# Projection work handed out in quarter pieces, and in another order, in a hybrid HGRN2 and SSD mixer

## The chip, the cores and the metric

The kernel runs on one core of a Trainium2 chip. Its engines run at the same time, each through its own list of instructions in order: TensorE (PE, with its weight loads shown as PEld), VectorE (DVE), ScalarE (ACT), GpSimd (POOL) and SyncE (SP, which here only issues DMAs). They wait for each other on semaphores. The metric is the device time of one execution in microseconds. Lower is better.

## The reference, cut to what matters

One layer, one sequence of L = 1024 latent tokens with 256 context tokens ahead of them, model width 1024. Everything starts from one projection of the modulated input:

```python
u = h @ w_in_l
aq, af_f, af_b, ai, ag, bz, bxbc, bdt_f, bdt_b, gate_a, gate_b = jnp.split(u, IN_SPLITS, axis=-1)
ya = hgrn2_branch(aq, af_f, af_b, ai, ag, ...)          # 4 heads, gated linear recurrence, both directions
yb = ssd_branch(bz, bxbc, bdt_f, bdt_b, ...)            # 4 groups of 4 heads, Mamba-2 scan, both directions
merged = jax.nn.sigmoid(gate_a) * (ya @ wpa) + jax.nn.sigmoid(gate_b) * (yb @ wpb)
return merged @ wo
```

The change lies mostly in the second branch. For one of its four groups:

```python
xbc = jax.nn.silu(dwconv_centred(xbc, conv_w, conv_b, n_rows))     # blocks x, B and C, 5 taps
u  = einsum('bktgn,bktgr,bktgrp->bkgrnp', bc, exp(cum_last - cum), x_dt)   # state each chunk adds
y  = einsum('bktgn,bktgr,bkgrnp->bktgrp', cc, exp(cum), s_prev)            # from earlier chunks
   + einsum('bktsg,bktsgr,bksgrp->bktgrp', cb, lmat, x_dt)                 # inside the chunk
y  = group_rms((y_f + y_b + d_skip * xh) * silu(z)) * norm_w               # norm of the group
```

All arithmetic is float32. A projection product is made of three products of halves, high by high, low by high and high by low.

## The kernel before

Channels lie on the 128 partitions and tokens along a row. A projection of 128 channels (`proj`, L196) runs over eight k-tiles for each part of the tokens: two parts of 512, and for some blocks a third part of 256 context tokens. With three products for each k-tile (`mm3`, L174, whose lines are L178 to L180) a part of 512 tokens is 24 products of 128x512. This text calls such a part a **grain**. `GRAIN` is its 512 tokens, and a part of 256 counts as half a grain.

The kernel has two long stages, the recurrence of the first branch (L697) and the scan of the second (L951), then the output products `pa`, `pb` and `fo`. In both stages two sorts of work share TensorE. The **scan** is a chain of small products between which the other engines work. The **fill** is a queue of projections that later work needs. Each is a Python generator. `Fill.window` (L93) steps the scan, adds up the weights that it yields times a rate, and steps the fill until what the fill yields has used that up. So the order in which the program is written alternates pieces of scan and of fill, and a piece of fill is as long as what the fill generator emits between two of its yields. `Fill.until(name)` (L88) runs the fill up to the end of a named entry without counting it against the rate. A scheduler then makes each engine's list from this order, with some instructions moved ahead (`ahead`), and where a ring of buffers has none free it puts the instruction later.

In the second stage each group g goes through `b_window` (L932). Its scan (`b_scan`, L761) transposes B (`bb`), makes the products of C and B (`cb`), transposes x (`bx`), makes nine state steps (`bu` on TensorE from `xw` on POOL, L808 to L811), and then 16 **y steps**. A y step, one half j of the group and one chunk t, goes through four stages (L837 to L870) which `LAGS` (L38) writes 0, 1, 2 and 4 steps late:

- `loads`: POOL issues the DMA of tile `L`, 256 KB from DRAM.
- `exponents`: POOL issues the DMA of tile `e`, 256 KB. DVE takes a minimum on `L` (L843). ACT makes four exponentials on it (L846).
- `products`: POOL multiplies `e` by C (L851). DVE multiplies `L` by `CB` (L852).
- `y_matmuls`: TensorE makes the eight products of the step (L867) from `L` and `e`.

The tiles `L` and `e`, the `xw` and the tiles of the norm take their buffers from one ring of 12 (`w2`, L716). `b_out` (L900) is the first half of the norm of the group before: it waits in the program for that group's z projections (`fill.until`), squares on ACT, adds on POOL (L909), sums over partitions on TensorE (`bss`, L913). `b_scale` (L919) is the second half, on DVE. `OUT1` and `OUT2` (L35) say after how many steps of the scan they stand. `FILL_B` (L34) is the rate of each group.

The fill of group g, in this order (L951 to L961): one `gb` block (the second branch's merge gate), the z blocks of group g-1, more `gb` blocks, and the four blocks B, C, x0 and x1 of group g+1. In grains, for g = 1 and 2: gb 2, z 4, B 2.5, C 2, x 5, together 15.5. Group 0 has 13.5 and group 3 has 16 (its own z comes last, in L962 to L967).

Of the kernel before, what the change touches and what calls it, by code (L numbers as in the profile page):

```python
# [33 lines left out]
FILL_B = (0.75, 0.86, 0.86, 0.93)  # L34
OUT1, OUT2 = 3, 4  # L35
# [68 lines left out]
def hybrid(tc, x, c, ctx, c_ctx, w_mod, b_mod, w_in, lb_logits, a_norm_w, conv_w, conv_b, dt_bias,  # L104
# [13 lines left out]
    with root:  # L118
# [77 lines left out]
        def proj(col, parts, name, w=None):  # L196

            hi, lo = w or w_col(col, name)
            for t0, n in parts:
                acc = pj(f"{name}_{t0}")  # L200
                mm3(acc[:, :n], [((hi[:, k, :], lo[:, k, :]), hsl(k, t0, n)) for k in range(KT)])
                yield t0, n, acc[:, :n]

        def proj_k(col, parts, name):
# [22 lines left out]
        with ExitStack() as st:  # L227
# [180 lines left out]
            for t0, n, acc in proj(0, parts_a[1:], "i0", w=w_i):  # L408
                iT0[t0] = get_kt(f"iT0_{t0}")
# [15 lines left out]
        def a_proj(h, u, pre=None):  # L425
            if pre is None:
                Tt = get_T(f"T{h}")
                for d, o in ((0, O_FF), (1, O_FB)):
                    for t0, n, acc in proj(o + h * P, parts_a, f"f{d}{h}"):
                        with ahead():  # L430
                            S.activation(Tt[:, d, t0:t0 + n], acc, AF.Sigmoid)
                        yield n / GRAIN
# [8 lines left out]
            for t0, n, acc in gen:  # L441
                if pre is None:
# [9 lines left out]
                yield n / GRAIN if pre is None else 0.1  # L452
            u["v"] = vt
            q = gt("q", 2, [L], f"q{h}")
            for t0, n, acc in proj(O_Q + h * P, parts_l, f"q{h}"):
                with ahead():
                    S.copy(q[:, t0:t0 + n], acc)
                yield n / GRAIN
            u["q"] = q

        def a_gate(h, u):
            for t0, n, acc in proj(O_G + h * P, parts_l, f"g{h}"):
                with ahead():
# [3 lines left out]
                yield n / GRAIN  # L467
# [116 lines left out]
        def gate_proj(o, dst, b, alloc, name, proj=proj):  # L584
            for t0, n, acc in proj(o + b * P, parts_l, f"{name}{b}"):
                with ahead():
# [3 lines left out]
                yield n / GRAIN  # L590
# [149 lines left out]
        def b_proj(g, u):  # L740
            xc = bt_("xc", 2, [2, L], f"xc{g}")
            xcc = bt_("xcc", 1, [2, LC], f"xcc{g}")
            Bc = bt_("bc", 3, [L], f"B{g}")
            Bcc = bt_("bcc", 1, [LC], f"Bc{g}")
            Cc = bt_("bc", 3, [L], f"C{g}")
            for blk, main, side in ((8 + g, Bc[:], Bcc[:]), (12 + g, Cc[:], None),
                                    (2 * g, xc[:, 0, :], xcc[:, 0, :]), (2 * g + 1, xc[:, 1, :], xcc[:, 1, :])):
# [344 lines left out]
```

## Time and profile before

| What | Value |
|---|---|
| Median of 3 runs | 1297.26 us (1296.8 to 1297.93) |
| The profiled execution's own time | 1292.7 us |
| Its span | 1290.9 us |
| PE busy | 1230.7 us (95%), mean granted clock 0.981 |
| DVE / ACT / POOL busy | 740.8 us (57%) / 547.2 us (42%) / 239.1 us (19%) |
| DMA | 137.01 MB, mean 106 GB/s |

The span is what the profile sees of the execution. Its own time has 1.8 us more around it, and the median of the runs shown lies 4.6 us above that one execution. Busy shares are means over stages that differ much, so the rows below cut the span into stages. PEclk is TensorE's granted clock as a share of 2.4 GHz. An arrow in a row reads out<-in by the names of the tiles. What stands in brackets at the end of a row is the idle time of the engine just before it, and what ended that.

### The profile page before, as it was taken

How to read it: one execution, taken by the hardware profiler on the slowest of the kernel's cores; microseconds unless marked ns; L12 is line 12 of the kernel's file. 1: busy time of each engine (PE TensorE's matmuls, PEld its weight loads, DVE VectorE, ACT ScalarE, POOL GpSimd, SP SyncE). 2: the span in 40 equal slices, each digit the busy share in tenths (PEclk: the TensorE clock that was granted, in tenths of full speed). 3: DMA queues.
4: the chain of work that ended last, by engine and by line, in shares of the span. 5: the costliest groups of instructions: out<-in, count | busy, mean ns of one | idle time of the engine just before them, and what ended most of it. 6: DMA issues, size and time to landing. Idle time of an engine off the chain costs nothing.

```text
span 1290.9 us, 18817 instructions
## 1 busy us (share of the span) xinstructions
PE 1230.7 (95%) x7624; PEld 1010.6 (78%) x7624; DVE 740.8 (57%) x988; ACT 547.2 (42%) x864; POOL 239.1 (19%) x264
## 2 busy tenths in 40 slices
PE   5999999999999999999889997999799979999997
PEld 2778888888888888887778886888688857888886
DVE  2427555833745723637762886288625665575568
ACT  2436344433343323334663556355646854312110
POOL 1220000000000000025520554066405560000000
PEclk8999999999999999999999998999899989999999
DMA  9511312112112222115631545145534655663312
GB/s 319 185 41 33 99 34 92 42 33 68 34 33 68 74 66 92 49 57 128 144 84 47 140 116 122 50 126 128 140 99 139 162 141 179 234 255 108 146 41 97
DMA packets 126837, 137.01 MB, mean 106 GB/s; under 512 B 15568, under 2 KB 102288, under 8 KB 126752
## 3 DMA queue, kind: packets, MB, share of 16 engines
q1 hardware_dynamic: 107744, 102.09, 25.2%
q0 software_dynamic: 18656, 33.69, 11.1%
q8 instruction: 60, 0.98, 0.3%
q14 instruction: 25, 0.20, 0.1%
q10 hardware_dynamic: 352, 0.05, 0.0%
HBM read 115.55 MB, written 20.19 MB: 105 GB/s over the span
## 4 chain that ended last, share of the span: by engine, by line
PE 76%; DVE 7%; issue 6%; POOL 5%; DMA 3%; ACT 1%; POOLq 0%; SPq 0%; DVEq 0%; ACTq 0%
PE f L180 3%; PE f L178 3%; PE x L178 3%; PE f L179 3%; PE x L179 3%; PE x L180 3%; PE pl L500 2%; POOL e L851 2%; PE z L178 2%; PE z L180 2%; PE pb L178 2%; PE pb L180 2%; PE fo L180 2%; PE fo L179 2%; PE z L179 2%
## 5 line engine op out<-in xcount | busy, mean ns | idle before, releaser
L851 POOL TENSOR_TENSOR e<-e,C 128x512 f32<-128x512 f32 x64 | 92.3, 1444 | 126.4 <-DMA e<-ecum_d 120.1
L846 ACT ACTIVATE L<-L,BIA 128x128 f32<-128x128 f32 x256 | 81.4, 390 | 58.6 <-DVE L L843 49.5
L808 POOL TENSOR_TENSOR xw<-xtc,WU 128x512 f32<-128x512 f32 x8 | 8.3, 1045 | 496.8 <-ACT xtc L794 496.8
L843 DVE TENSOR_TENSOR L<-L,CU 128x512 f32<-128x512 f32 x64 | 52.6, 823 | 51.3 <-DMA L<-cum_d 32.0
L867 PE MATMUL yi<-L,xt 128*64 128x128 f32 x512 | 42.7, 290 | 26.5 <-issue 15.0
L867 PEld LDWEIGHTS yi<-L,xt 128*64 128x64 f32 x512 | 29.5, 141 | 37.8 <-issue 20.6
L726 DVE SCALAR_TENSOR_TENSOR xc<-x,par,xc 128x496 f32<-128x496 f32 (+1 forms) x64 | 47.0, 734 | 18.5 <-ACT xc L723 17.7
L852 DVE TENSOR_TENSOR L<-L,CB 128x512 f32<-128x512 f32 x64 | 54.3, 855 | 3.9 <-ACT L L846 3.9
L178 PE MATMUL fo<-wo,mh 128*128 128x512 f32 x128 | 50.2, 392 | 0.0
L867 PE MATMUL yi<-e,St 128*64 128x128 f32 x512 | 42.6, 290 | 7.7 <-POOL e L851 5.8
L180 PE MATMUL fo<-wo,mh 128*128 128x512 f32 x128 | 49.8, 389 | 0.0
L179 PE MATMUL fo<-wo,ml 128*128 128x512 f32 x128 | 49.8, 389 | 0.0
L492 ACT COPY KX<-K 128x1024 f32<-128x1024 f32 x28 | 31.9, 1140 | 41.2 <-DVE K L511 40.4
L511 DVE TENSOR_TENSOR K<-K,T 128x1280 f32<-128x1280 f32 x28 | 46.4, 1658 | 3.5 <-ACT KX L492 1.6
L542 DVE SCALAR_TENSOR_TENSOR S<-S,T,ub 128x128 f32<-128x128 f32 x64 | 22.2, 348 | 43.6 <-PE ub L532 23.6
L898 DVE TENSOR_TENSOR xc<-xc,z 128x512 f32<-128x512 f32 x16 | 13.2, 825 | 55.2 <-ACT z L887 55.1
L833 POOL DMA_DIRECT2D e<-ecum_d x64 | 39.5, 617 | 8.3 <-PE yi L867 8.2
L503 DVE COPY_PREDICATED PD<-mk,pl 128x512 f32<-128x512 uint8 x24 | 17.7, 739 | 39.3 <-PE pl L500 25.6
L867 PEld LDWEIGHTS yi<-e,St 128*64 128x64 f32 x512 | 32.5, 146 | 9.4 <-POOL e L851 7.4
L513 DVE TENSOR_TENSOR Q<-Q,T 128x1024 f32<-128x1024 f32 x28 | 37.6, 1344 | 3.2 <-PE pl L500 3.2
L833 POOL DMA_DIRECT2D L<-cum_d x64 | 39.3, 614 | 1.0 <-PE bu L811 0.6
L500 PEld LDWEIGHTS pl<-Q,KX 128*64 128x64 f32 x896 | 30.1, 138 | 9.2 <-issue 8.7
(996 smaller groups left out, 3766.1 us busy)
## 6 DMA issues: line engine op xcount, KB each, us to landing
L<-cum_d POOLq DMA_DIRECT2D x64, 256.0 KB, 5.5
e<-ecum_d POOLq DMA_DIRECT2D x64, 256.0 KB, 5.2
wm<-in_w_mod_dram SPq DMA_DIRECT2D x16, 512.0 KB, 7.9
xt<-in_x_dram SPq DMA_DIRECT2D x8, 512.0 KB, 7.6
ga_d<-ga SPq DMA_DIRECT2D x16, 256.0 KB, 2.1
gb_d<-gb SPq DMA_DIRECT2D x16, 256.0 KB, 2.0
m<-ga_d SPq DMA_DIRECT2D x8, 512.0 KB, 6.1
gbt<-gb_d SPq DMA_DIRECT2D x8, 512.0 KB, 7.4
```

What stands on the lines that cost most here:

```text
L178: T.matmul(dst, ah, bh, start=(first and i == 0), stop=False)
L179: T.matmul(dst, al, bh, start=False, stop=False)
L180: T.matmul(dst, ah, bl, start=False, stop=(last and i == n - 1))
L500: T.matmul(pl[rows_, t * HP:(t + 1) * HP], KX[:, o:o + HP], qx, start=True, stop=True)
L511: V.tensor_tensor(kv, kv, sub(Ta, lv, [[w, NA // w], [NA - lv, 2], [0, lv]]), ALU.mult)
L726: V.scalar_tensor_tensor(d3[:, :, a:z], r3[:, :, a + o:z + o], cw_col(t, blk), d3[:, :, a:z], ALU.mult, ALU.add)
L833: G.dma_start(t_[:].rearrange("p a b c -> p (a b c)"), bass.AP(src.tensor, src.offset, [[NQT * BH * 2 * QT, REP], [0, P // REP], [1, 4 * Q ...
L843: V.tensor_tensor(Lm, Lm, sub(CU[:], t * BH + h0, [[1, 2], [NT * BH, 2], [0, P]]), ALU.min)
L846: S.activation(Lm[:, h, d, :], Lm[:, h, d, :], AF.Exp, bias=BIA[:, d, t, h0 + h:h0 + h + 1])
L851: G.tensor_tensor(C4, C4, Cc[:, ts].unsqueeze(1).broadcast_to([P, 4, P]), ALU.mult)
L852: V.tensor_tensor(Lm, Lm, CB[:, :, ts].unsqueeze(1).broadcast_to([P, 2, 2, P]), ALU.mult)
L867: T.matmul(yi[h * 64:(h + 1) * 64, o], a, r, start=(k == 0), stop=(k == 3))
```

## The change

Four things change. First, `proj` yields after every second k-tile, so a grain leaves the queue in four pieces of six products. The last z block, made by `proj_k`, yields likewise. Every user of a projection passes these yields on and counts a quarter of a grain for each. Second, the fill of a group has another order: B and C of the next group, z of the group before, the `gb` blocks, then x0 and x1 of the next group. `b_proj` takes its tiles when the first part of a block is done, not all at the start. Third, the norm of the group before stands after 8 steps of the scan and not 3, and its second half 3 steps later and not 4. Fourth, the rates of the four groups go from 0.75, 0.86, 0.86 and 0.93 to 0.74, 0.64, 0.64 and 0.8.

```diff
-FILL_B = (0.75, 0.86, 0.86, 0.93)
-OUT1, OUT2 = 3, 4
+FILL_B = (0.74, 0.64, 0.64, 0.8)
+OUT1, OUT2 = 8, 3
...
                 acc = pj(f"{name}_{t0}")
-                mm3(acc[:, :n], [((hi[:, k, :], lo[:, k, :]), hsl(k, t0, n)) for k in range(KT)])
+                for k in range(KT):
+                    mm3(acc[:, :n], [((hi[:, k, :], lo[:, k, :]), hsl(k, t0, n))], first=(k == 0), last=(k == KT - 1))
+                    if k % 2 and k < KT - 1:
+                        yield t0, n, None
                 yield t0, n, acc[:, :n]
...
             for t0, n, acc in proj(O_G + h * P, parts_l, f"g{h}"):
+                if acc is None:
+                    yield n / GRAIN / 4
+                    continue
...
-                yield n / GRAIN
+                yield n / GRAIN / 4
...
         for g in range(BG):
-            add_gb(1)
+            if g + 1 < BG:
+                fill.add(b_proj(g + 1, ub_[g + 1], ("B", "C")), f"b{g + 1}")
+            else:
+                add_gb(1)
             if g:
                 fill.add(z_proj(g - 1, ub_[g - 1]), f"z{g - 1}")
-            add_gb(GATES[g] - 1)
+            add_gb(GATES[g] - (g + 1 == BG))
             if g + 1 < BG:
-                fill.add(b_proj(g + 1, ub_[g + 1]), f"b{g + 1}")
+                fill.add(b_proj(g + 1, ub_[g + 1], ("x0", "x1")), f"b{g + 1}")
```

What this does to the lists of the engines is shown at three places of group 1. In the names, `L1_0_3` is the tile `L` of group 1, half 0, chunk 3, `e1_0_3` the tile `e` of the same step, and the last number is a buffer's.

TensorE at the first y steps, before: the end of a part of x4, three y steps in a row, and the next part, of which the first product is shown.

```order
L180 MATMUL x4_512_5932<-hl7_96,x4h_5865 128x512
L867 MATMUL yi1_0_0_5973<-L1_0_0_5862,xt1_5483 64x128 x4
L867 MATMUL yi1_0_0_5973<-e1_0_0_5903,St1_5664 64x128 x4
L867 MATMUL yi1_0_0_5973<-L1_0_1_5901,xt1_5483 64x128 x4
L867 MATMUL yi1_0_0_5973<-e1_0_1_5912,St1_5664 64x128 x4
L867 MATMUL yi1_0_0_5973<-L1_0_2_5910,xt1_5483 64x128 x4
L867 MATMUL yi1_0_0_5973<-e1_0_2_5923,St1_5664 64x128 x4
L178 MATMUL x4_1024_6020<-hc0_97,x4h_5865 128x256
```

And now:

```order
L180 MATMUL x4_0_5888<-hl5_94,x4h_5883 128x512
L902 MATMUL yi1_0_0_5929<-L1_0_0_5845,xt1_5454 64x128 x4
L902 MATMUL yi1_0_0_5929<-e1_0_0_5855,St1_5531 64x128 x4
L178 MATMUL x4_0_5888<-hh6_87,x4h_5883 128x512
L179 MATMUL x4_0_5888<-hh6_87,x4l_5884 128x512
L180 MATMUL x4_0_5888<-hl6_95,x4h_5883 128x512
L178 MATMUL x4_0_5888<-hh7_88,x4h_5883 128x512
L179 MATMUL x4_0_5888<-hh7_88,x4l_5884 128x512
L180 MATMUL x4_0_5888<-hl7_96,x4h_5883 128x512
L902 MATMUL yi1_0_0_5929<-L1_0_1_5853,xt1_5454 64x128 x4
L902 MATMUL yi1_0_0_5929<-e1_0_1_5873,St1_5531 64x128 x4
```

Every y step now has a quarter of a grain behind it, where three steps stood in a row with a whole part between such rows.

POOL at the same y steps, before: `DMA` rows are the loads it issues, the others its products.

```order
L851 TENSOR_TENSOR e1_0_0_5903<-e1_0_0_5903,C1_4637 128x512
L851 TENSOR_TENSOR e1_0_1_5912<-e1_0_1_5912,C1_4637 128x512
L833 DMA L1_0_3_5921<-cum_d_79 128x1x512
L833 DMA e1_0_2_5923<-ecum_d_80 128x1x512
L833 DMA L1_0_4_5962<-cum_d_79 128x1x512
L833 DMA e1_0_3_5964<-ecum_d_80 128x1x512
L851 TENSOR_TENSOR e1_0_2_5923<-e1_0_2_5923,C1_4637 128x512
L851 TENSOR_TENSOR e1_0_3_5964<-e1_0_3_5964,C1_4637 128x512
```

And now:

```order
L886 TENSOR_TENSOR e1_0_0_5855<-e1_0_0_5855,C1_4625 128x512
L868 DMA e1_0_2_5897<-ecum_d_80 128x1x512
L886 TENSOR_TENSOR e1_0_1_5873<-e1_0_1_5873,C1_4625 128x512
L868 DMA L1_0_4_5918<-cum_d_79 128x1x512
L868 DMA e1_0_3_5920<-ecum_d_80 128x1x512
L886 TENSOR_TENSOR e1_0_2_5897<-e1_0_2_5897,C1_4625 128x512
L868 DMA L1_0_5_5951<-cum_d_79 128x1x512
L868 DMA e1_0_4_5953<-ecum_d_80 128x1x512
L886 TENSOR_TENSOR e1_0_3_5920<-e1_0_3_5920,C1_4625 128x512
```

Before, the load of e1_0_2 and its product have no other product between them; now the load stands one product earlier.

POOL ahead of the first load of group 1, before: the adds of the norm of group 0 (`sq`) and the nine `xw`, of which the last five follow the four shown in the same way.

```order
L909 TENSOR_TENSOR sq0_0_0_5646<-sq0_0_0_5646,sq0_0_1_5647 128x512
L808 TENSOR_TENSOR xw1_0_5665<-xtc1_5484,WU_106 128x512
L909 TENSOR_TENSOR sq0_1_0_5655<-sq0_1_0_5655,sq0_1_1_5656 128x512
L808 TENSOR_TENSOR xw1_1_5702<-xtc1_5484,WU_106 128x512
L808 TENSOR_TENSOR xw1_2_5709<-xt1_5483,WU_106 128x512
L808 TENSOR_TENSOR xw1_3_5716<-xt1_5483,WU_106 128x512
```

And now, the last rows ahead of the first load and that load:

```order
L947 TENSOR_TENSOR sq0_0_0_5759<-sq0_0_0_5759,sq0_0_1_5760 128x512
L843 TENSOR_TENSOR xw1_5_5783<-xt1_5454,WU_106 128x512
L843 TENSOR_TENSOR xw1_6_5796<-xt1_5454,WU_106 128x512
L947 TENSOR_TENSOR sq0_1_0_5768<-sq0_1_0_5768,sq0_1_1_5769 128x512
L843 TENSOR_TENSOR xw1_7_5812<-xt1_5454,WU_106 128x512
L843 TENSOR_TENSOR xw1_8_5832<-xt1_5454,WU_106 128x512
L868 DMA L1_0_0_5845<-cum_d_79 128x1x512
```

The second add, which needs all z blocks of group 0, stood seven `xw` and more ahead of the first load and now stands two ahead of it.

## Rows read from the trace of the kernel before

**Rows 1.** Windows: stretch, length, busy PE, PEld, DVE, ACT, POOL, clock, DMA.

```profile
583.00:667.30 84.30, 75.21 (x520) 61.59 (x519) 63.44 (x91) 47.55 (x93) 40.25 (x49) 0.96 0.57 128
667.30:724.20 56.90, 56.90 (x287) 47.78 (x283) 23.30 (x32) 26.15 (x37) 12.82 (x12) 1.00 0.18 56
724.20:802.20 78.00, 69.02 (x504) 58.34 (x503) 64.79 (x93) 50.06 (x96) 41.47 (x49) 0.93 0.60 142
802.20:853.80 51.60, 51.60 (x252) 42.81 (x248) 17.53 (x23) 20.60 (x31) 13.04 (x12) 1.00 0.16 51
853.80:931.80 78.00, 69.53 (x505) 58.50 (x503) 64.42 (x93) 48.66 (x95) 44.36 (x49) 0.93 0.62 142
931.80:986.90 55.10, 55.10 (x267) 45.69 (x264) 16.89 (x19) 30.59 (x40) 13.63 (x12) 1.00 0.31 96
986.90:1064.30 77.40, 69.74 (x474) 56.36 (x472) 50.91 (x62) 50.00 (x96) 42.66 (x49) 0.94 0.61 164
1064.30:1290.90 226.60, 217.66 (x950) 177.87 (x948) 143.62 (x183) 49.07 (x64) 1.28 (x1) 0.99 0.42 151
```

**Rows 2.** Waits of POOL: engine, tile, line, releaser, total us, times, longest.

```profile
POOL e L851 <- DMA e<-ecum_d: 120.1, 53, 6.6
POOL e L833 <- PE yi L867: 8.2, 4, 3.1
POOL e L851 <- DVE C L726: 3.8, 1, 3.8
```

**Rows 3.** The page's costliest groups: count, busy, mean ns of one, idle before.

```profile
L851 POOL TENSOR_TENSOR e<-e,C 128x512 f32<-128x512 f32 x64 | 92.3, 1444 | 126.4 <-DMA e<-ecum_d 120.1
L833 POOL DMA_DIRECT2D e<-ecum_d x64 | 39.5, 617 | 8.3 <-PE yi L867 8.2
```

**Rows 4.** POOL in order of time, three places: start us, length, instruction.

```profile
726.52 0.63 POOL L833 DMA_DIRECT2D e<-ecum_d  x1
...
734.32 1.27 POOL L851 TENSOR_TENSOR e<-e,C 128x512 f32<-128x512 f32 x1 [1.02 <-DMA e<-ecum_d]
...
736.15 0.61 POOL L833 DMA_DIRECT2D e<-ecum_d  x1
...
741.30 1.27 POOL L851 TENSOR_TENSOR e<-e,C 128x512 f32<-128x512 f32 x1 [3.37 <-DMA e<-ecum_d]
...
1025.26 0.63 POOL L833 DMA_DIRECT2D e<-ecum_d  x1
...
1026.46 0.62 POOL L833 DMA_DIRECT2D e<-ecum_d  x1
...
1029.70 1.35 POOL L851 TENSOR_TENSOR e<-e,C 128x512 f32<-128x512 f32 x1 [2.03 <-DMA e<-ecum_d]
1032.75 1.29 POOL L851 TENSOR_TENSOR e<-e,C 128x512 f32<-128x512 f32 x1 [1.70 <-DMA e<-ecum_d]
```

**Rows 5.** POOL in order of time, the norm's second add of group 0.

```profile
710.79 1.54 POOL L909 TENSOR_TENSOR sq<-sq,sq 128x512 f32<-128x512 f32 x1 [3.43 <-ACT sq L908]
712.29 1.04 POOL L808 TENSOR_TENSOR xw<-xtc,WU 128x512 f32<-128x512 f32 x1
```

**Rows 6.** TensorE in order of time: a fill, three y steps and a fill.

```profile
617.12 0.39 PE L179 MATMUL x<-hh,x13l 128*128 128x512 f32 x1
617.34 0.39 PE L180 MATMUL x<-hl,x13h 128*128 128x512 f32 x1
617.66 0.66 PE L867 MATMUL yi<-L,xt 128*64 128x128 f32 x8
...
619.90 0.61 PE L867 MATMUL yi<-e,St 128*64 128x128 f32 x8
...
620.77 0.40 PE L179 MATMUL x<-hh,x2l 128*128 128x512 f32 x1
```

**Rows 7.** TensorE in order of time: z's last product in group 1; two state steps.

```profile
707.92 0.39 PE L180 MATMUL z<-hl,z1h 128*128 128x512 f32 x1
...
721.64 1.02 PE L811 MATMUL bu<-xw,btc 128*128 128x256 f32 x4
722.50 1.89 PE L811 MATMUL bu<-xw,bt 128*128 128x256 f32 x8
```

More of the change, by code (lines that the diff above doesn't have):

```diff
@@ L441, in a_proj @@
             for t0, n, acc in gen:
+                if acc is None and pre is None:
+                    yield n / GRAIN / 4
+                    continue
                 if pre is None:
@@ L451, in a_proj @@
                 S.copy(vt[:, t0 // P:(t0 + n) // P, :], tv[:, :n].rearrange("p (a b) -> p a b", b=P))
-                yield n / GRAIN if pre is None else 0.1
+                yield n / GRAIN / 4 if pre is None else 0.1
             u["v"] = vt
@@ L462, in a_gate @@
             for t0, n, acc in proj(O_G + h * P, parts_l, f"g{h}"):
+                if acc is None:
+                    yield n / GRAIN / 4
+                    continue
                 with ahead():
@@ L585, in gate_proj @@
             for t0, n, acc in proj(o + b * P, parts_l, f"{name}{b}"):
+                if acc is None:
+                    yield n / GRAIN / 4
+                    continue
                 with ahead():
@@ L738, in silu_now, with b_proj @@
                 S.activation(v, v, AF.Silu)
[L740 to L747, printed above, removed]
-                for t0, n, acc in proj(O_X + blk * P, parts_l if side is None else parts_a, f"x{blk}"):
-                    dst = main[:, t0:t0 + n] if t0 < L else side
-                    conv(acc, n, dst, blk, ROW if t0 < L else LC, f"x{blk}_{t0}")
+        def b_proj(g, u, names):
+            blks = dict(B=8 + g, C=12 + g, x0=2 * g, x1=2 * g + 1)
+            for name in names:
+                blk = blks[name]
+                main = side = None
+                for t0, n, acc in proj(O_X + blk * P, parts_l if name == "C" else parts_a, f"x{blk}"):
+                    if acc is None:
+                        yield n / GRAIN / 4
+                        continue
+                    if name in "BC":
+                        if t0 == 0:
+                            u[name] = bt_("bc", 3, [L], f"{name}{g}")
+                        elif t0 == L:
+                            u["Bc"] = bt_("bcc", 1, [LC], f"Bc{g}")
+                        main, side = u[name][:], u["Bc"][:] if t0 == L else None
+                    else:
+                        j = int(name[1])
+                        if j == 0 and t0 == 0:
+                            u["xc"] = bt_("xc", 2, [2, L], f"xc{g}")
+                        elif j == 0 and t0 == L:
+                            u["xcc"] = bt_("xcc", 1, [2, LC], f"xcc{g}")
+                        main, side = u["xc"][:, j, :], u["xcc"][:, j, :] if t0 == L else None
+                    conv(acc, n, main[:, t0:t0 + n] if t0 < L else side, blk, ROW if t0 < L else LC, f"x{blk}_{t0}")
                     silu_now()
@@ L942, in hybrid @@
         ub_ = [{} for _ in range(BG)]
-        fill.add(b_proj(0, ub_[0]), "b0")
+        fill.add(b_proj(0, ub_[0], ("B", "C", "x0", "x1")), "b0")
         fill.until("b0")
```

22 lines of the change are left out of this document (16 added, 6 removed).

## The prediction, written before the changed kernel ran

> **What bounds the kernel now.** I read the stages first, as windows [rows 1]. The second stage alternates two kinds of stretch. A **Y stretch** goes from POOL's first `L` load of a group to the group's last y product (rows of 84.3, 78.0, 78.0 and 77.4 us). A **P stretch** goes from there to the next first load (56.9, 51.6, 55.1). In a P stretch PE is busy all the time at full clock: only less work, or work elsewhere, shortens it. In a Y stretch PE is idle for 7.7 to 9.1 us and its clock is 0.93 to 0.96, so something else sets the pace. The waits name it: POOL stood 120.1 us, 53 times, at the product `e` times C for the DMA of `e` [rows 2]. Its 64 products take 1.444 us each and its `e` loads 0.617 us each [rows 3]; 16 products and 32 loads are 23.1 + 19.7 = 42.8 us of a Y stretch of 78.
>
> How late a load is depends on the loads issued just ahead of it. In time order [rows 4] the first of a burst is used 4.44 us after its issue began, the second 5.15, the third 6.29, the fifth 7.8; I put the fourth at 7.0, between its neighbours. So POOL's list in the Y stretches can be walked by hand: loads 0.61 us each, a product when POOL is free and its own load has landed.
>
> **Y stretches.** Before, four loads (L, e, L, e) are followed by two products. The first `e` is issued at 0.6 and lands at 5.8, its product ends at 7.2; the second, fourth of the burst, is issued at 1.85, lands at 8.85, and its product ends at 10.3. That is 5.15 us a step. Now the pattern is L, next e, product. The next `e` has one product between its issue and its use, so the period T obeys T = (0.6 + 5.15 - T) + 1.44, or 3.6 us. Not every step has the new pattern: of the 16 products of a group, 7, 7, 7 and 6 had no other product between their load and themselves, and now 8, 2, 2 and 5. Walked in full, the lists give 72.2, 73.2, 73.2 and 69.2 us before, and 77.7, 62.5, 62.5 and 67.8 now. The walk of before is sound: its idle time (these less 42.8 each) is 116.6 us against the measured 120.1. The measured stretches are longer than the walk by 12.1, 4.8, 4.8 and 8.2 us, from what the walk leaves out: POOL's waits on PE and DVE, and the last y products behind fill.
>
> For now I add 1.8 us to each. That is the smallest excess of before, 4.8, less 3.0, which is a quarter of POOL's waits on PE and on DVE's `C` (8.2 + 3.8 us) [rows 2]. They come from whole grains and whole blocks placed between steps, and those are cut in four or moved. The ends are 0 each (7.2 us less) and the old excess (22.7 more). So the Y stretches become 79.5, 64.3, 64.3 and 69.6: -4.8, -13.7, -13.7 and -7.8, together **-40.0 us**.
>
> PE should not take POOL's place there. A half y step takes (619.90 - 617.66) / 5 = 0.45 us, a whole one 0.9, and fill products start 0.22 us apart [rows 6], so a grain of 24 is 5.3 us. From 617.34 to 620.77 the three steps took 3.43 us, 0.3 more than 3 x 0.9 + 2 x 0.22: that is one change from fill to scan and back. A step of group 1 or 2 has 0.27 grain behind it: 0.9 + 1.4 + 0.3 = 2.6 us against POOL's 62.5 / 16 = 3.9. The extra changes in a Y stretch (114 round trips in the second stage against 57) lie under that difference; if PE were the pace they would cost 0.3 us each.
>
> **P stretches.** Here the fill comes back, since no part of it goes away. Before, group 1's z was done 6.5 grains into the P stretch. Its last product ends at 708.15, 40.85 us after 667.3 [rows 1, 7]; 6.5 grains are 34.3, so `bb`, `cb` and `bx` are 6.5. Now z is behind B and C of the next group, 9.75, 8.75 and 6.25 grains after the last y of the group before: 51.5, 46.2 and 33.0 us. Five state steps, 0.86 each [rows 7], make 4.3. Then the change holds up the loads: the norm's second add stands two `xw` ahead of the first load. That add ended at 712.25, 4.1 us after z, and an `xw` takes 1.04 [rows 5]: z to first load is 4.1 + 2.1 = 6.2. So a P stretch is now its grains + 6.5 + 4.3 + 6.2 = 68.5, 63.2 and 50.0 against 56.9, 51.6 and 55.1: +11.6, +11.6, -5.1, or **+18.1 us**. If the add's wait let the load past, 6.2 would go three times; if ACT is later with its squares, as much again could be lost. Before, the add was hidden under seven `xw` whose buffers were not yet needed; that cover is gone.
>
> **Tail and start.** Of the last group's own z, 39 products, and of `pa` 20, ran before the last y and now come after it: 59 x 0.22 = 13.0, and two round trips of 0.3 for the sums of the norm: **+13.6** on the 226.6 of the last window [rows 1], where PE is busy for 217.7 us and nothing hides it. At the first stage's end of the queue the finer pieces give 15 more round trips, 0 to 0.3 us each, taken at half (+2.2), and a quarter of a grain less ahead of group 0's `bx` (-1.3): **+0.9**.
>
> The sum is -40.0 + 18.1 + 13.6 + 0.9 = **-7.4 us**. The profiled execution took 1292.7 us, span 1290.9, and so would take 1285.3. It lies 4.6 us below the median of 1297.26, so the median goes to **1289.9 us**, -0.6%.
>
> **Rivals.** *The Y stretches keep their excess* (slower). The walk knows only `e`. A step also needs `L`, by a minimum and a product on DVE and four exponentials on ACT. DVE is busy 64.8 of 78.0 us in group 1 and 50.9 of 77.4 in group 3, which has no next group's blocks to filter [rows 1]. With B and C's part of that filtering (half of the difference) gone to the P stretch it needs about 57 of the 64.3 that I give it: 89%, and any bunching makes it the bound. With the whole old excess the sum is -7.4 + 22.7 = +15.3, **1312.6 us**. It decides from an excess of 3.7 us a stretch (14.6 / 4), where the gain is gone; I have put 1.8, and the smallest measured is 4.8, which speaks for it. Against it: two of the old four had 8 and 4 us at their ends or starts that smaller pieces should shorten.
>
> The products on POOL took 1.27 to 1.35 us in the rows in time order and 1.444 on the mean [rows 3, 4], so some are stretched by something. The Trainium skill ("Advanced Engine Details and Errata", section "GPSIMD Details") says that POOL shares a read and a write interface with DVE and conflicts with DVE instructions that have two SBUF inputs; DVE's own product of `L` by `CB` is such a one. By that rule a DVE that is busier by share would stretch them more: at the 1.54 us of the longest POOL row shown [rows 5], 64 x 0.1 = 6.4 us would be lost, and the sum would be -1.0. No row separates the two inputs from anything else, so I leave it out of the sum.
>
> *The loads land sooner* (faster still). With fewer loads at once the second would be like the first, 4.4, the third 5.15 and so on. The walk is then 72.7, 58.3, 58.3 and 63.2, which is 18.0 less: **1271.9 us**. For it: the time rises with the position in the burst. Against: 4 loads of 256 KB for two steps become 4 in less time, so the queues are as full.
>
> *The clock.* In the Y stretches it is already below full [rows 1], and PE will have many small gaps, one a step. PE decides from a mean clock of 2.6 / 3.9 = 0.67; at 0.6 a step takes 4.3 us, 0.4 x 16 = 6.9 a stretch, in two stretches 13.9: **1304 us**. Against: it was 0.93 with gaps of the same sum. The Trainium skill ("TensorE: Matmul & The Clock Gate", section "A second HAM failure mode: psum-queue depth-cycling") tells that small idle times between groups of products make the clock go to and fro between its two levels, so that throughput falls though single products are at full speed. The 0.93 is in line with some of that and not with much.
>
> *Nothing is won.* PE is busy 95% and all its work stays; where PE is the true bound, work only moves between the stretches: **1297 us**, give or take 2. Against it is the 34 us that PE idles in the four Y stretches.
>
> **How the numbers follow.** A measurement of this kernel can tell about 0.2%, 2.6 us, from no change. Chances: the forecast 0.42 (its own range 1283 to 1297, most of which is over 2.6 us faster: 0.34 faster, 0.08 same), excess kept 0.27 (1300 to 1313), loads sooner 0.15 (1271 to 1283), clock 0.07, nothing won 0.09. So faster 0.34 + 0.15 = 0.49, same 0.08 + 0.09 = 0.17, slower 0.34. For 8 in 10 I leave out the outer half of the loads that land sooner and the top of the excess: 1276 to 1309.
>
> **What would show it.** Each step has its stretch in the windows: first `L` load to last y at about 79, 64, 64 and 70 us; the P stretches at about 68, 63 and 50, with the second add of the norm right ahead of the loads; the last window at 240. POOL's wait for the DMA of `e` should fall to about 99 us (the walk's idle time, 34.9 + 19.7 + 19.7 + 25.0). If it falls and the Y stretches do not, the wait has gone to `L` on DVE or ACT. If it stays, the landing time grew with the rate of loads. PE idle of well over 14 us in Y1 would say that I have its work too large; a clock below 0.8 would say that the gaps count. The forecast is wrong if the sum of the four Y stretches is over 295 us (317.7 before), whatever the others do.

## The result, and the profile after

The changed kernel takes 1307.23 us (median of 7 runs, 1304.17 to 1312.56), the kernel before 1296.8 us (7 runs, 1288.55 to 1297.93). The ratio of the means is 1.0103, with a 95% interval of 1.0071 to 1.0135: 1% slower, where 0.6% faster was forecast.

The profiled execution has a span of 1302.8 us against 1290.9. Its stages stand below as in [rows 1]: Y and P stretches by turns, the last window being the tail. The columns are again stretch, length, busy PE, PEld, DVE, ACT and POOL, clock, and DMA.

```profile
579.30:656.80 77.50, 73.61 (x504) 56.93 (x502) 52.51 (x73) 45.08 (x89) 40.65 (x48) 1.00 0.55 143
656.80:726.00 69.20, 68.77 (x346) 57.80 (x346) 38.58 (x56) 27.61 (x40) 12.18 (x12) 1.00 0.17 46
726.00:797.50 71.50, 60.38 (x438) 46.50 (x436) 56.44 (x68) 42.11 (x88) 42.29 (x48) 0.93 0.65 155
797.50:861.10 63.60, 63.17 (x315) 52.92 (x316) 32.86 (x48) 26.96 (x38) 12.13 (x12) 1.00 0.15 42
861.10:933.40 72.30, 61.74 (x438) 47.54 (x437) 52.90 (x68) 43.32 (x89) 42.52 (x49) 0.93 0.62 161
933.40:983.30 49.90, 49.43 (x243) 41.00 (x244) 21.58 (x29) 24.66 (x34) 12.13 (x12) 1.00 0.28 85
983.30:1062.10 78.80, 70.71 (x459) 53.27 (x458) 45.82 (x53) 50.86 (x96) 41.68 (x49) 0.94 0.61 158
1062.10:1302.80 240.70, 231.04 (x1007) 188.57 (x1007) 146.58 (x188) 51.32 (x68) 2.56 (x2) 0.99 0.42 148
```

| Part | Before | Forecast | After |
|---|---|---|---|
| Start, to the first `L` load | 583.0 | +0.9 | 579.3 (-3.7) |
| Y stretches | 84.3, 78.0, 78.0, 77.4 | 79.5, 64.3, 64.3, 69.6 | 77.5, 71.5, 72.3, 78.8 (-17.6 in sum, forecast -40.0) |
| P stretches | 56.9, 51.6, 55.1 | 68.5, 63.2, 50.0 | 69.2, 63.6, 49.9 (+19.1, forecast +18.1) |
| Tail | 226.6 | +13.6 | 240.7 (+14.1) |

What the change puts into the P stretches and the tail came as worked out. Of what it was to take from the Y stretches, 22 us did not come. The sum of the column is +11.9, the difference of the spans.

POOL's waits and the groups of the y step, beside [rows 2, 3]. First the lines of the kernel before that [rows 2, 3] do not have, waits and then one group:

```profile
ACT L L846 <- DVE L L843: 49.5, 24, 6.3
DVE L L843 <- DMA L<-cum_d: 32.0, 16, 10.5
PE yi L867 <- DVE L L852: 10.0, 8, 3.2
```

```profile
L852 DVE TENSOR_TENSOR L<-L,CB 128x512 f32<-128x512 f32 x64 | 54.3, 855 | 3.9 <-ACT L L846 3.9
```

And after:

```profile
POOL e L886 <- DMA e<-ecum_d: 100.6, 47, 4.2
ACT L L881 <- DVE L L878: 87.7, 39, 5.3
DVE L L878 <- DMA L<-cum_d: 51.7, 26, 3.9
PE yi L902 <- DVE L L887: 21.8, 10, 4.9
```

```profile
L886 POOL TENSOR_TENSOR e<-e,C 128x512 f32<-128x512 f32 x64 | 92.7, 1448 | 107.5 <-DMA e<-ecum_d 100.6
L878 DVE TENSOR_TENSOR L<-L,CU 128x512 f32<-128x512 f32 x64 | 51.1, 800 | 70.4 <-DMA L<-cum_d 51.7
L887 DVE TENSOR_TENSOR L<-L,CB 128x512 f32<-128x512 f32 x64 | 66.3, 1051 | 6.0 <-ACT L L881 5.9
```

POOL's wait for `e` fell from 120.1 us to 100.6; the walk had given 99. So POOL does what was forecast, and the y steps still come late. TensorE now waits 21.8 us for DVE's product of `L` (10.0 before), which takes 1051 ns on the mean (855 before). The waits for `L` ahead of it grew too: DVE's for the load from 32.0 to 51.7 us, ACT's for DVE's minimum from 49.5 to 87.7. POOL's last product of a group ends 75.4, 66.4, 63.8 and 70.6 us into the stretches, near the walk's 77.7, 62.5, 62.5 and 67.8; the last y product ends 2, 5, 8 and 8 us after it.

The end of group 2's Y stretch shows how. DVE, POOL and PE in order of time:

```profile
914.98 0.68 DVE L878 TENSOR_TENSOR L<-L,CU 128x512 f32<-128x512 f32 x1
916.27 1.07 DVE L878 TENSOR_TENSOR L<-L,CU 128x512 f32<-128x512 f32 x1 [0.61 <-issue]
917.26 0.68 DVE L887 TENSOR_TENSOR L<-L,CB 128x512 f32<-128x512 f32 x1
921.84 0.69 DVE L878 TENSOR_TENSOR L<-L,CU 128x512 f32<-128x512 f32 x1 [3.90 <-DMA L<-cum_d]
922.44 1.51 DVE L749 SCALAR_TENSOR_TENSOR xc<-x,par,xc 128x496 f32<-128x496 f32 x2
923.87 1.56 DVE L887 TENSOR_TENSOR L<-L,CB 128x512 f32<-128x512 f32 x1
```

```profile
915.38 1.41 POOL L886 TENSOR_TENSOR e<-e,C 128x512 f32<-128x512 f32 x1 [1.96 <-DMA e<-ecum_d]
916.73 0.63 POOL L868 DMA_DIRECT2D L<-cum_d  x1
...
922.27 2.61 POOL L886 TENSOR_TENSOR e<-e,C 128x512 f32<-128x512 f32 x2 [2.46 <-DMA e<-ecum_d]
```

```profile
925.48 1.12 PE L902 MATMUL yi<-L,xt 128*64 128x128 f32 x8 [3.85 <-DVE L L887]
```

Counted from 0, the last load of `L`, of step 15, is issued at 916.73, behind a product that had waited for its `e`. Its minimum stands in DVE's list ahead of the product of step 13, so that product waits until the load lands at 921.84. Then two filter taps pass, and then it takes 1.56 us and not 0.68, while POOL makes its own products beside it (922.27 to 924.9; what the two do to each other is shown further below). TensorE, ready for step 13 since about 921.6, starts it at 925.48.

### The profile page after: what moved, and what is told of

Read it like the earlier page. It is cut to its first block, busy times and chain, and to the rows that moved or that the text cites. A ratio compares the mean times of both kernels' runs of the same rounds, so it can differ in the third digit from the quotient of the medians.

```text
span 1302.8 us, 18836 instructions
## 1 busy us (share of the span) xinstructions
PE 1241.5 (95%) x7624; PEld 1004.4 (77%) x7624; DVE 752.9 (58%) x988; ACT 533.9 (41%) x851; POOL 236.8 (18%) x264
## 3 DMA queue, kind: packets, MB, share of 16 engines
q0 software_dynamic: 18656, 33.69, 10.8%
## 4 chain that ended last, share of the span: by engine, by line
PE 69%; issue 14%; POOL 7%; DVE 4%; DMA 3%; ACT 2%; SPq 0%; POOLq 0%; DVEq 0%; ACTq 0%
PE x L178 4%; PE x L179 3%; PE x L180 3%; POOL e L886 3%; PE f L180 3%; PE f L178 3%; PE f L179 2%; PE ga L178 2%; PE pl L520 2%; PE fo L179 2%; PE fo L180 2%; PE fo L178 2%; PE ga L180 2%; PE ga L179 2%; PE pb L178 2%
## 5 line engine op out<-in xcount | busy, mean ns | idle before, releaser
L881 ACT ACTIVATE L<-L,BIA 128x128 f32<-128x128 f32 x256 | 81.6, 391 | 88.0 <-DVE L L878 87.7
L886 POOL TENSOR_TENSOR e<-e,C 128x512 f32<-128x512 f32 x64 | 92.7, 1448 | 107.5 <-DMA e<-ecum_d 100.6
L878 DVE TENSOR_TENSOR L<-L,CU 128x512 f32<-128x512 f32 x64 | 51.1, 800 | 70.4 <-DMA L<-cum_d 51.7
L902 PE MATMUL yi<-L,xt 128*64 128x128 f32 x512 | 44.3, 296 | 28.5 <-DVE L L887 21.8
L887 DVE TENSOR_TENSOR L<-L,CB 128x512 f32<-128x512 f32 x64 | 66.3, 1051 | 6.0 <-ACT L L881 5.9
L902 PEld LDWEIGHTS yi<-L,xt 128*64 128x64 f32 x512 | 28.2, 142 | 51.6 <-DVE L L887 28.3
L520 PE MATMUL pl<-Q,KX 128*64 128x64 f32 x896 | 34.1, 230 | 0.7 <-DVE Q L533 0.7
```

Of the source, the lines that this page charges most:

```text
L520: T.matmul(pl[rows_, t * HP:(t + 1) * HP], KX[:, o:o + HP], qx, start=True, stop=True)
L878: V.tensor_tensor(Lm, Lm, sub(CU[:], t * BH + h0, [[1, 2], [NT * BH, 2], [0, P]]), ALU.min)
L881: S.activation(Lm[:, h, d, :], Lm[:, h, d, :], AF.Exp, bias=BIA[:, d, t, h0 + h:h0 + h + 1])
L886: G.tensor_tensor(C4, C4, Cc[:, ts].unsqueeze(1).broadcast_to([P, 4, P]), ALU.mult)
L887: V.tensor_tensor(Lm, Lm, CB[:, :, ts].unsqueeze(1).broadcast_to([P, 2, 2, P]), ALU.mult)
L902: T.matmul(yi[h * 64:(h + 1) * 64, o], a, r, start=(k == 0), stop=(k == 3))
```

## The experiments

Ratios are to the kernel before, run beside each, taken from the means, with 95% intervals. Stretches and waits are those of one profiled execution, and executions of one kernel differ: eight of a_nomin took 1293.8 to 1302.4 us, and the profiled one was the longest. The first four ask which part of the change costs.

**Whole pieces, all else new** (a_whole): in `proj`, and likewise in the last z block and in what each piece counts for,

```diff
-                    if k % 2 and k < KT - 1:
-                        yield t0, n, None
```

> The changed kernel with the pieces of a projection whole again (24 products between two yields); order of the fill, place of the norm and rates stay new. PE then goes from fill to scan and back 151 times, against 228 in the changed kernel and 156 in the one before. Theory 1, each such change costs PE about 0.15 us of busy time (10.8 us more PE busy for 72 more): some 11 us less than the changed kernel, 1294 of its 1304.6 profiled, PE busy about 1231. Theory 2, the y steps wait for L by way of DVE and ACT, and pieces of fill have no part in it: within 3 us of the changed kernel, 1302 to 1308. Theory 3, the fill that went from the Y stretches to the P stretches and the tail is what costs, pieces help: slower than the changed kernel, 1306 to 1315, Y stretches longer by 3 or more each.

1317.87 us, 1.0197 (1.0159 to 1.0235). **Half pieces** (a_halves), with `if k == KT // 2 - 1:`:

> The changed kernel with pieces of twelve products (two to a grain) in place of six. 188 changes from fill to scan, between 151 and 228. Theory 1: 40 x 0.15 = 6 us less than the changed kernel, about 1298.5, PE busy about 1235.5. Theory 2: 1302 to 1308. Theory 3: 1304 to 1309, between the two piece sizes beside it.

1320.20 us, 1.0211 (1.0175 to 1.0248).

**Quarter pieces alone** (b_quarters), the order of the fill as before too (only the tiles of a block are still taken late):

```diff
-FILL_B = (0.74, 0.64, 0.64, 0.8)
-OUT1, OUT2 = 8, 3
+FILL_B = (0.75, 0.86, 0.86, 0.93)
+OUT1, OUT2 = 3, 4
```

> The kernel before with the quarter pieces alone: order of the fill, place of the norm and rates are those of before (tiles of the blocks B, C and x are still taken when a part is done). 215 changes from fill to scan against 156. Theory 1: 59 x 0.15 = 9 us more than before, 1302 against 1292.7 profiled, PE busy about 1240. Theory 2: no cost of their own, and the y steps bunch less; 1285 to 1293. Theory 3: the same, 1285 to 1293, since the fill stays where it was.

1328.73 us, 1.0278 (1.0232 to 1.0323).

**Old rates** (a_rates), the line of `FILL_B` in the diff above alone.

> The changed kernel with the rates of before (0.75, 0.86, 0.86, 0.93). 218 changes from fill to scan. Theory 1: 10 x 0.15 = 1.5 us less, about 1303. Theory 2 and 3: more fill goes into the Y stretches, where PE is idle for 8 to 11 us in each of the last three, and less is left for the P stretches and the tail; up to the 14 us by which the tail grew come back, 1291 to 1298, with the last window at 227 to 233.

1299.08 us, 1.0052 (1.0033 to 1.0070).

The first three times lie above what any of the theories expected. Theory 1 falls: 151 changes from fill to scan were slower than 228. Theory 2 falls as it stood, since the size of the pieces did matter. Theory 3 holds for the rates alone (tail 231.7). New order with old pieces and new pieces with old order are each worse than both together. The walk, done for these lists afterwards, gives that for b_quarters and a_halves, and not for a_whole. Here it is for all kernels with the loads on POOL that leave nothing out, summed over the four groups: the walk of POOL's list, the measured end of POOL's last product, and the Y stretches to the modelled end of the last y product.

| Kernel | Walk | Last product | Y stretches |
|---|---|---|---|
| before | 287.8 | 303 | 318 |
| changed | 270.5 | 276 | 300 |
| a_whole | 274.7 | 300 | 329 |
| a_halves | 299.1 | 304 | 320 |
| b_quarters | 332.6 | 341 | 358 |
| a_rates | 297.3 | 293 | 311 |
| a_split | 246.7 | 266 | 283 |
| b_split | 279.0 | 295 | 315 |

Between the walk and POOL's last product lie -4 to 25 us, so the walk ranks most of the kernels and does not give their times. In b_quarters 11, 11 and 12 products of groups 1 to 3 stand right behind their own load, and the walk gives 85, 85 and 87 where POOL's last product ended at 84, 84 and 93. POOL there, in order of time:

```profile
771.28 1.92 POOL L886 TENSOR_TENSOR e<-e,C 128x512 f32<-128x512 f32 x1 [3.31 <-DMA e<-ecum_d]
773.14 0.62 POOL L868 DMA_DIRECT2D e<-ecum_d  x1
773.76 0.59 POOL L868 DMA_DIRECT2D L<-cum_d  x1
779.87 1.25 POOL L886 TENSOR_TENSOR e<-e,C 128x512 f32<-128x512 f32 x1 [5.52 <-DMA e<-ecum_d]
```

8.6 us for one step, since the load goes out only when the product before it is done.

**POOL's product one step later** (a_split): TensorE's list is the same.

```diff
-LAGS = (0, 1, 2, 4)
+LAGS = (0, 1, 2, 3, 4)
...
-                for lag, stage in zip(LAGS, (loads, exponents, products, y_matmuls)):
+                for lag, stage in zip(LAGS, (loads, exponents, products, e_products, y_matmuls)):
```

> The changed kernel with one stage of a y step taken apart: POOL's product of e by C comes one step later than DVE's product of L by CB (0, 1, 2, 3, 4 steps late). Only POOL's list changes: a product of e then has two others between its load and itself. Theory A (a Y stretch lasts as long as POOL's list takes, by its loads' landing times): the walk gives 73.7, 54.1, 54.1 and 64.8 in place of 77.7, 62.5, 62.5 and 67.8; POOL's last products come earlier by 3 to 8 us, its wait for e falls from 100 to about 76, the time by some 15 to 24 us to 1281 to 1290. Theory B (the y steps are held by L, that is its load, DVE's minimum, ACT's exponentials and DVE's product): POOL waits less, but the Y stretches keep 77.6, 71.6, 72.3 and 78.8 within 3 us and the time 1300 to 1308.

1285.07 us, 0.9942 (0.9921 to 0.9963): some 1.6% off the changed kernel by moving POOL's products (the scheduler moved 13 instructions in DVE's list with them). The Y stretches (columns as above), the two products and DVE's minimum:

```profile
580.90:661.40 80.50, 75.67 (x504) 58.49 (x503) 51.40 (x73) 44.98 (x89) 40.67 (x48) 0.96 0.58 138
730.60:795.80 65.20, 58.71 (x437) 44.96 (x436) 53.83 (x69) 41.98 (x87) 41.69 (x48) 0.97 0.67 171
859.30:925.30 66.00, 57.88 (x438) 44.15 (x437) 52.01 (x69) 43.03 (x89) 40.62 (x49) 1.00 0.71 177
975.20:1046.60 71.40, 67.69 (x458) 50.93 (x458) 45.22 (x52) 50.25 (x96) 41.99 (x48) 0.98 0.68 170
```

```profile
L890 POOL TENSOR_TENSOR e<-e,C 128x512 f32<-128x512 f32 x64 | 90.3, 1414 | 90.2 <-DMA e<-ecum_d 84.0
L885 DVE TENSOR_TENSOR L<-L,CB 128x512 f32<-128x512 f32 x64 | 53.9, 849 | 7.9 <-ACT L L881 7.9
L878 DVE TENSOR_TENSOR L<-L,CU 128x512 f32<-128x512 f32 x64 | 59.6, 935 | 58.0 <-DMA L<-cum_d 37.9
```

Groups 1 to 3 lost 6 to 7 us each, and group 0 gained 3. POOL waits 17 us less (theory A), though its last products came 10.5 us sooner in sum and not the walk's 23.8. DVE's product is back from 1051 to 849 ns, with 17 and not 26 of the 64 overlapping a product of POOL by 0.3 us or more. DVE's minimum, which also reads two tiles of SBUF, went from 800 to 935 ns in exchange, so DVE's two instructions together got only 4 us lighter. TensorE's wait for the product fell from 21.8 to 9.1 us. The same edit on the kernel before (b_split):

> The kernel before with POOL's product of e one step after DVE's product of L, as in the changed kernel with that edit, where it gave 19 us. The walk of POOL's list: 70.5, 71.9, 71.9, 64.7 in place of 72.2, 73.2, 73.2, 69.2, in sum 8.8 us less; so 1284 to 1291 on a kernel before at 1293 if the walk is what counts. If what the edit gave there was that DVE's and POOL's products no longer ran side by side, then here too DVE's product gets shorter than its 0.855 us, and it may give more.

1288.39 us, 0.9958 (0.9940 to 0.9976), in the range that the walk gave; DVE's product took 830 ns in place of 855.

**Loads on SP** (a_sp), in `rows`:

```diff
-                G.dma_start(t_[:].rearrange("p a b c -> p (a b c)"),
+                nc.sync.dma_start(t_[:].rearrange("p a b c -> p (a b c)"),
```

> The changed kernel with the loads of L and e issued by SP in place of POOL, so that no load stands behind a product that waits. TensorE's list is the same but for places of pieces that the scheduler moves. Theory A: POOL has only its products left, 23 us of a Y stretch; the Y stretches fall to what PE and DVE need, 58 to 68 each, the time to 1265 to 1285. Theory B: as the loads of L come earlier too, L is late only by DVE and ACT: Y stretches of 66 to 74, 1285 to 1300. A third way: SP issues weights and the stores of the gates as well and stands waiting at these; then the loads come later, and the time is over 1310.

1277.18 us, 0.9870 (0.9836 to 0.9904). So nothing on SP held the loads up enough to undo the gain. Y stretches:

```profile
575.50:651.30 75.80, 75.80 (x517) 59.45 (x515) 52.64 (x75) 46.20 (x92) 24.81 (x19) 1.00 0.47 154
...
717.80:784.30 66.50, 61.05 (x445) 46.41 (x443) 47.76 (x68) 44.76 (x91) 26.59 (x19) 0.97 0.51 175
...
845.30:911.50 66.20, 60.74 (x445) 46.46 (x443) 48.16 (x68) 45.73 (x92) 26.39 (x19) 0.97 0.54 183
...
958.80:1029.80 71.00, 68.22 (x466) 51.28 (x464) 41.37 (x52) 52.47 (x99) 24.48 (x19) 1.00 0.54 178
```

PE idles 14 us in the four, against 34 in the changed kernel. The edit also moves the loads to another kind of queue: nearly all of the 33.69 MB of the queue q0, software_dynamic, go to q1, hardware_dynamic. That they land faster there is not the reason: where POOL waited for its `e`, the product began 5.2 us (median) after the load was issued in the changed kernel, and 7.9 us after it here. The later ones are issued sooner: a group's last load of `e` goes out 57.7, 53.0, 52.8 and 62.2 us into the stretches, against 70.2, 61.1, 58.1 and 64.5. The same on the kernel before, and with quarter pieces alone:

> The kernel before with the loads of L and e issued by SP in place of POOL. Theory A (in both kernels a Y stretch is as long as POOL's list with its loads takes): PE's idle time in the four Y stretches, 34 us, falls by half or more, the time to 1270 to 1280, as far below before as the changed kernel with loads on SP lies below the changed one. Rival: with whole grains the y steps still come in bunches behind fill, and the loads on SP stand behind the stores of the gates; 1285 to 1295.

> The kernel before with quarter pieces, and with the loads on SP. With the loads on POOL the quarter pieces alone cost 36 us. Theory A: that was POOL's list alone (11 to 12 products a group right behind their own load); it is gone here, and the time is that of the kernel before with loads on SP within 5 us. Rival, the changes from fill to scan (99 against 55 in the second stage, 0.15 us each): 6 to 9 us above it. If the 36 us stay in half or more, the pieces themselves hold up something else, and theory A falls.

1284.52 us, 0.9930 (0.9905 to 0.9954), and 1289.03 us, 0.9969 (0.9947 to 0.9992). For the kernel before, theory A missed: PE's idle time in the Y stretches fell from 34 to 28 us and not by half, and the time lies at the edge of what the rival expected. What holds its Y stretches then was not looked into. The 36 us of the quarter pieces are down to 4.5, so nearly all of them were POOL's list with the loads in it. And with the loads out of it the whole change pays: 1277.18 against 1284.52, -0.6%, the two intervals just apart.

**Versions that follow** (ar_sp, old rates and loads on SP; a_sp_split and ar_sp_split, the later product on top):

> The changed kernel with the loads on SP and the rates of before. The tail falls from 240.8 to about 232 and the P stretches by 4 us, as the rates did with the loads on POOL; the Y stretches grow by 11 us if PE is what they wait for now, by less if not. Theory A with PE as the next bound: 1273 to 1278, no gain on the new rates; if PE idle in Y still has room: 1264 to 1272.

> The changed kernel with the loads on SP and POOL's product one step after DVE's. DVE's product takes 0.68 us where POOL makes no product beside it and up to 2.6 where it does. If what is left in the Y stretches is these two together, DVE's product goes from 0.81 us on the mean to under 0.75 and the time falls by 3 to 8 us, to 1269 to 1274; if it is PE, no change, 1275 to 1279.

> The changed kernel with the loads on SP, the rates of before, and POOL's product one step after DVE's. Without the last edit it took 1269.9 us; on top of the loads on SP the edit gave 1.4 us with the new rates, inside the noise. If TensorE is the bound now: 1267 to 1272.

1269.91 us, 0.9825 (0.9780 to 0.9869); 1275.76 us, 0.9877 (0.9821 to 0.9933); 1269.30 us, 0.9824 (0.9799 to 0.9849). The old rates bring the tail back to 232, and the Y stretches of groups 1, 2 and 3 grow by 2, 3 and 8 us. The later product gives nothing more that can be measured: DVE's product stayed at 812 ns (806 in a_sp), where under 750 and 3 to 8 us less were expected. ar_sp beats both kernels; it is the changed kernel with the line of `rows` and the line of rates.

**What makes L late.** Six kernels leave work out. TensorE's and POOL's lists stay as they were but for what is left out and a few places, but the scheduler also moved other instructions in DVE's list, so not every other instruction kept its place: by the order in the traces 14 in a_nolcb, 20 in a_noconv, 26 in a_nomin, 3 in a_nodve, 66 in a_two and 48 in a_sp_two. Without DVE's product (a_nolcb, the first line below), and without the side taps of x0 and x1 (a_noconv, the others):

```diff
-                V.tensor_tensor(Lm, Lm, CB[:, :, ts].unsqueeze(1).broadcast_to([P, 2, 2, P]), ALU.mult)
...
-                for t, o in ((0, -2), (1, -1), (3, 1), (4, 2)):
+                for t, o in ((0, -2), (1, -1), (3, 1), (4, 2)) if blk >= 8 else ():
```

> The changed kernel without DVE's product of L by CB (left out of the computation); every other instruction keeps its place. Theory A: POOL's last products stay where they are (75.4, 66.4, 63.8, 70.6 us into the stretches), the time falls by 3 us at most. Theory B: DVE is 66 us lighter and L ready 1 to 2 us sooner in each step; the time from POOL's last product to the last y, 2.2, 5.2, 8.5 and 8.2 us, falls to 2 to 4 each, the sum of the Y stretches by 12 to 20 us. If POOL's products get shorter too (1.448 us on the mean), the two engines hold each other up when both read tiles.

> The changed kernel without the four side taps of the filter of the blocks x0 and x1 (left out of the computation), which are DVE's other work in the Y stretches of groups 0 to 2; every other instruction keeps its place. Theory A: no change beyond 3 us. Theory B, with DVE's share of busy time as the cause: the end of the stretches of groups 1 and 2 comes 5 to 8 us sooner, group 3, which has no such work, stays at 78.8.

1.0036 (1.0014 to 1.0059) and 1.0141 (1.0104 to 1.0178). Without the product the Y stretches are 8 us shorter in sum, where 12 to 20 were expected, and the time some 0.7% below the changed kernel's. Without the taps, as much DVE work (some 60 us), they are not shorter but 9 us longer (83.2, 76.1, 71.8 and 78.4). So a smaller busy share of DVE alone gains nothing here.

With two products in place of three in the fill of the Y stretches (a_two, and a_sp_two with the loads on SP), `mid` being false for x2 to x7:

```diff
-                T.matmul(dst, al, bh, start=False, stop=False)
+                if mid:
+                    T.matmul(dst, al, bh, start=False, stop=False)
```

> The changed kernel with two products in place of three for each k-tile of the blocks x0 and x1 of groups 1 to 3 (low by high is left out of the computation). These are the fill of the Y stretches of groups 0 to 2, so TensorE has about 30 products or 6.6 us less up to the 15th y step of groups 1 and 2, which in the changed kernel ends 68.9 and 69.6 us after the first load. POOL's list by the walk: 61.2 in place of 62.5. If TensorE's work is the bound: 62 to 63. If POOL and L are: 67 to 70. Group 3, whose fill is whole, stays at 75.5.

> The same left out, with the loads issued by SP. With loads on SP the 15th y step of groups 1 and 2 ended 63.8 and 63.6 us after the first load, and TensorE was idle for 5 us of the whole stretch. If TensorE is the bound there: 57 to 59. If it is the y steps' own chain (loads, DVE, ACT, POOL's products): 61 to 64.

1.0135 (1.0095 to 1.0174) and 0.9804 (0.9769 to 0.9839). Both bounds of the expectation missed: the 15th step of groups 1 and 2 ended at 76.5 and 78.8 us, not sooner but 8 and 9 us later, though POOL's last products ended at 64.9 and 65.5. On SP it was 67.5 and 70.0, later as well; the gain there lies in the P stretches. So less work on TensorE did not shorten a Y stretch in these two. What TensorE waited for in a_two:

```profile
PE yi L904 <- DVE L L889: 46.5, 13, 7.6
```

Why that wait grew from 21.8 us when TensorE had less to do was not settled; DVE's and ACT's lists were changed too by the scheduler there.

Without DVE's minimum (a_nomin), and without minimum and product (a_nodve, where the product's line goes as well):

```diff
-                V.tensor_tensor(Lm, Lm, sub(CU[:], t * BH + h0, [[1, 2], [NT * BH, 2], [0, P]]), ALU.min)
...
-                        S.activation(Lm[:, h, d, :], Lm[:, h, d, :], AF.Exp, bias=BIA[:, d, t, h0 + h:h0 + h + 1])
+                        S.activation(Lm[:, h, d, :], Lm[:, h, d, :], AF.Exp, bias=epsr, scale=0.0)
```

> The changed kernel without DVE's minimum on L (left out, and the exponentials get a scale of 0 and a constant for their bias, so that they stay finite). TensorE's and POOL's lists are the same. If L is late because the minimum of a later step, waiting for its load, stands ahead of the product of an earlier step in DVE's list: TensorE's wait for the product falls from 21.8 us to under 10, the Y stretches of groups 1 to 3 from 71.6, 72.3 and 78.8 to about 66, 67 and 73, the time by 10 to 17 us. If the load, ACT or the stretched product is what is late: the stretches stay within 3 us, as ACT then waits for the load in its own list.

> The changed kernel without the minimum and without DVE's product of L by CB (both left out, exponentials as in the run beside it). A y step then needs POOL's product and ACT's exponentials alone. If POOL's list is the bound once L is early: the Y stretches end 2 to 4 us after POOL's last product, at about 78, 69, 66 and 73, and POOL's last products stay at 75.4, 66.4, 63.8 and 70.6. If they shrink below that, it was DVE's instructions that stretched POOL's.

1.0035 (1.0015 to 1.0054) and 0.9986 (0.9967 to 1.0006). a_nomin: the wait for the product fell to 14.4 us and not under 10, group 3 to 71.4, groups 1 and 2 stayed (70.9, 72.9), and group 0 grew to 84.6. So the sum stayed at 299.8, and of what the theory of DVE's order asked only group 3 came; the time fell by some 0.7%. a_nodve, Y stretches and POOL's product:

```profile
579.20:659.90 80.70, 75.68 (x504) 58.16 (x502) 28.99 (x40) 45.09 (x89) 39.29 (x49) 0.98 0.54 138
729.00:794.40 65.40, 59.09 (x438) 44.28 (x437) 25.97 (x36) 42.29 (x88) 39.14 (x49) 1.00 0.69 170
858.00:922.60 64.60, 59.60 (x438) 45.20 (x437) 25.52 (x37) 42.24 (x88) 39.83 (x48) 0.97 0.68 177
972.50:1043.30 70.80, 66.40 (x459) 50.00 (x458) 16.29 (x20) 50.54 (x96) 39.70 (x49) 1.00 0.65 172
```

```profile
L885 POOL TENSOR_TENSOR e<-e,C 128x512 f32<-128x512 f32 x64 | 83.3, 1303 | 113.3 <-DMA e<-ecum_d 107.0
```

In sum 281.5 us against 300.1, and against 277.7 of the forecast; the time is some 1.2% below the changed kernel's. With DVE's two instructions gone, all four stretches are what the forecast had (79.5, 64.3, 64.3 and 69.6) within 1.2 us.

## Why the prediction was wrong

**The step that failed** is the excess of the Y stretches over the walk: "For now I add 1.8 us to each", on the ground that it came from whole grains between the steps. It measured 29.6 us in sum (77.5, 71.5, 72.3 and 78.8 less 270.5), the 29.9 of before nearly unchanged. That is the first rival, with its price: it gave 1312.6 us for the whole old excess, and would have given 1308 with the start as measured. Its sign came too, as the prediction had named it: POOL's wait fell, and the wait had gone to `L`. By its own limit of 295 us for the four stretches the forecast was wrong.

That the two sums agree is chance, for the excess had changed its place. Up to POOL's last products it fell from 15 to 6 us (25 in a_whole, whose grains are whole), in line with the prediction's reason. Behind them it was put at nothing and rose from 15 us, 10 of them in group 0, to 24, of which 5 to 8 lie in each of groups 1 to 3. 18.6 of the 29.6 us go with DVE's minimum and product (300.1 to 281.5), 4 of them ahead of POOL's last products and the others behind. So the walk lacked the second input of a y step. `L` is loaded by the same queue, its minimum and product wait in DVE's list in order, and both can run beside POOL's product.

The rival's reason was half right. It named `L` and DVE, but by DVE's busy share, and without the taps DVE was lighter to no effect. Two things are at work in the rows at the end of group 2: a minimum that waits for its load ahead of a product that could run, and the two products at one time. How the 18.6 us divide between these two, and the mere length of DVE's two instructions, is open: a_nolcb and a_nomin take 8 and less than 1 us from the sum when done singly, and group 0 alone differs by up to 7 us between kernels with the same lists of TensorE and POOL.

**The walk** held for the changed kernel. It missed POOL's last products by 6 us in 270 and foresaw POOL's wait for `e` (99, measured 100.6). Of the other runs it misses a_whole by 25 us and a_split by 19; that whole grains between the steps cause the 25 is argued and not shown. The walk fell by 17.3 us and the stretches by 17.6. The other 22 of the 40 were the excess that was to go.

**TensorE not the bound** held as far as a_two and a_sp_two can tell: with fewer products the stretches did not shrink. The extra changes from fill to scan were put at nothing in the Y stretches. PE busy is 1241.5 us in the changed kernel with 228 of them and 1230.7 before with 156, but 1230.2 in a_sp, which has the same 228: so they need not cost anything, and the 11 us are not theirs. **The P stretches and the tail** were right within 1 us each, the second add of the norm included: it starts at 722.18, and the first load of group 1 follows two `xw` later at 725.92 [rows 5]. **The start** was put at +0.9 and came -3.7; why is open.

**The clock** stayed at 0.93 in groups 1 and 2 as before, so that rival did not come about.

**POOL and DVE on each other.** Left out of the sum for want of a row, this is now shown. The view of the tile `L` in the changed kernel has the shortest, median and longest time of DVE's product (ns):

```profile
L887 DVE TENSOR_TENSOR L<-L,CB x64: 674/686/2571, 594.2 to 1052.7; 128x512 f32<-128x512 f32 x64
```

Set against POOL's products in the same trace, it takes 0.683 us in the 36 cases with no product of POOL beside it, and 1.587 on the mean of the 26 that overlap one by 0.3 us or more (up to 2.571). In 22 of these 26 it ends 0.55 or 0.56 us after POOL's product, however long they overlap; in the other four it takes 0.68 us, and POOL's product ends 1.12 to 1.15 us after it. So here one waits for the other, rather than both being slow. The minimum, also with two inputs in SBUF, takes 0.686 alone and 0.938 on the mean of 28. The filter taps, which read PSUM and one tile of SBUF, do not change: 0.733 and 0.728 us for those of 128x496, 0.741 and 0.738 for 128x504. POOL's product takes 1.303 us without DVE's two (a_nodve) and 1.448 with them, 64 x 0.145 = 9.3 us. The Trainium skill ("Advanced Engine Details and Errata", section "GPSIMD Details") says that POOL shares a read and a write interface with DVE and conflicts with DVE instructions that have two SBUF inputs; the traces agree, on both sides of it. The prediction weighed that rule for POOL's product alone; DVE's product pays more, 64 x (1.051 - 0.683) = 23.6 us of DVE time, part of it in the chain of a y step. How much of that reaches the time is not shown.

## What to carry to other kernels

An operation with two inputs needs a walk for each: shortening the chain of one shows the other, and an excess over a walk should not be taken off before its own instructions are found. Loads that stand in the list of an engine which also waits for them are paced by that wait; issued by SP, they made the same change worth 0.6%, where it had cost 1%. When two engines make products from SBUF for the same step, try them a step apart: that gave 1.6% here with the loads on POOL, and nothing measurable with the loads on SP.

## What was not expected of the hardware

DVE's products with two SBUF inputs more than double beside a product on POOL (0.683 to 1.587 us), as one of the two waits for the other to end, while its taps, with one input in PSUM, do not change (0.733 and 0.728). A queue of loads moved from POOL to SP took its 0.61 us an issue out of POOL's list (POOL busy 236.8 to 160.8 us). Each load then took longer from issue to use (7.9 us in place of 5.2 where POOL waited for it), and the kernel was still 2.3% faster than the changed one.
